# First modulation weights in four chunks of columns, with the first row pair multiplied chunk by chunk, in a hybrid encoder layer

## Chip, cores and metric

One core of one Trainium2 chip. The metric is device time in microseconds (us) from start to end of one launch of the whole layer; the median of three runs of the kernel before is 2013.69 us (2010.76 to 2014.69).

## What is computed

Two sequences (s = 0, 1) of 1024 rows by 1024 columns go through one encoder layer. What matters here is its beginning:

```
mod = silu(c) @ w_ada + b_ada                     # c: one vector of 1024 per sequence, w_ada: 1024 x 6144
sh1, sc1, ga1, sh2, sc2, ga2 = split(mod, 6)
h = rmsnorm(x, g_mix) * (1 + sc1) + sh1           # 1024 x 1024
z = h @ w_in                                      # to 448 latent columns (q_lat, kv_lat, k_pe) and 512 Fourier columns
...                                               # latent attention, 2-D Fourier mixing, w_out, residual, SwiGLU FFN
```

No row of `z` can be made before `sh1` and `sc1` are there, and these take the first 2048 columns of `w_ada`: 8 MB. All arithmetic is in float32. Matrix products are made from high and low parts with three matmuls each (`mm3`, lines 79 to 81).

## The kernel before

The whole kernel is one program. The order of the work on each engine is the order in which the program issues it, except where a scheduler moves an instruction forward; `tc.issue_after(x)` and `behind()` hold an instruction back until `x`, or the last split, was issued. SyncE (SP) issues almost all loads of this part in one queue, strictly in order: a load that waits for its buffer holds back all loads after it. TensorE (PE), VectorE (DVE), ScalarE (ACT) and GpSimd (POOL) also keep their order. Tiles with the same `tag` share a buffer, so a load into a tag waits until the earlier tile's readers are done.

The part that is changed is the opening, up to the second pair of row blocks:

- **Modulation.** `mod_load(c, ...)` loads rows 128c to 128c+127 of the first 2048 columns of `w_ada` (1 MB, eight times), and `mod_mm(0, c, ...)` makes four matmuls of 512 columns from it, one for each group of 512 columns (L233). They add over c, so the result is complete only when the eighth block is in. Then `modrow` is copied from PSUM (L655), four transposes (L160) turn it into columns, and `mod_vecs` (L163, L166) makes the scales `s1` and the shifts `sh1`.
- **Weights folded meanwhile.** Between the loads, `fold_q`, `fold_out` (L269, L270), `prep_wcs` (L352 to L362, the Fourier weights `wcs`) and `wz_split` prepare weights.
- **First pair (k = 0).** A pair is 128 rows and their 128 partners. `norm(k)` squares the rows on ACT (L383), takes the inverse root on POOL (`rstd`, six small operations, L104 to L111) and scales the rows on DVE (L396). `flip(k, g)` transposes two blocks of 128 columns of both row blocks (L424), and ACT applies `s1` and `sh1` (L431). For k = 0 the result is split into `hh` and `hl`, and `zproj` multiplies both row blocks by `wz` (24 matmuls of 448 columns each). `evenodd` makes sums and differences of the two row blocks on POOL (L452) and splits them; `fourier_in(k, 0)` and `fourier_in(k, 1)` multiply them by `wcs` (24 matmuls of 280 columns, 24 of 256).
- **Second pair (k = 1).** It is flipped between the parts of the first; `latents` transposes the first pair's normalised latents (L538); then `zboth(1)` multiplies sum and difference by `wz` (i = 0, 24 matmuls; i = 1, 24 matmuls). Between these two lie the transposes of the inverse roots of the third pair (L404, in `prepare`).

Of the kernel before, what the change touches and what calls it, by code (L numbers as in the profile page):

```python
# [12 lines left out]
F32 = mybir.dt.float32  # L13
# [40 lines left out]
def hybrid_encoder_kernel(ctx: ExitStack, tc: tile.TileContext, a: dict):  # L54
# [72 lines left out]
    s1 = [edge.tile([P, NC], F32, name=f"s1_{s}") for s in range(2)]  # L127
    sh1 = [const.tile([P, NC], F32, name=f"sh1_{s}") for s in range(2)]
# [51 lines left out]
    with ExitStack() as st:  # L180
# [14 lines left out]
        wuqT = w.tile([P, HEADS, QL], F32, tag="hh0", name="wuqT")  # L195
        wq = w2.tile([P, 4, 512], F32, tag="wada", name="wq", bufs=2).rearrange("p a b -> p (a b)")[:, :1536].rearrange("p (a b) -> p a b", a=2)
# [31 lines left out]
        def mod_mm(key, c, wt):  # L228
            if c == 0:
                mods[key] = bank()  # L230
            for n, j in enumerate((2, 3, 0, 1)):
                with tc.issue_after(here["m"]) if n else ExitStack():
                    here["m"] = nc.tensor.matmul(  # L233
                        mods[key][32 * j : 32 * j + 32, :], scT[:, c, :], wt[:, j, :], start=(c == 0), stop=(c == NC - 1)).ins

# [149 lines left out]
        def norm(k):  # L385
# [9 lines left out]
            for u in range(2):  # L395
                nc.vector.tensor_scalar(out=xt[u], in0=xt[u], scalar1=r[:, u : u + 1], scalar2=None, op0=ALU.mult)  # L396

# [13 lines left out]

        def flip(k, g):
            s, j = pairs[k]
            if g == 0:
                st1["hf", k] = w3.tile([P, NC, 2, P], F32, tag="hf", name="hf", bufs=1)
                if k == 0:
                    st1["hh", k] = w.tile([P, NC, 2, P], F32R, tag="hh0", name="hh")
                    st1["hl", k] = w.tile([P, NC, 2, P], F32R, tag="hl0", name="hl")
            hf, xt = st1["hf", k], st1["x", k]
            pt = bank().rearrange("p (c u t) -> p c u t", c=2, u=2)  # L420
            for c in range(2):
                for u in range(2):
                    cc = 2 * g + c
                    nc.tensor.transpose(pt[:, c, u, :], xt[u][:, cc * P : (cc + 1) * P], ident)  # L424
            for c in range(2):
                cc = 2 * g + c
                if k == 0 and cc == 1:
                    nc.vector.tensor_scalar(out=hf[:, cc], in0=pt[:, c], scalar1=s1[s][:, cc : cc + 1],
                                            scalar2=sh1[s][:, cc : cc + 1], op0=ALU.mult, op1=ALU.add)
                    continue  # L430
                nc.scalar.activation(hf[:, cc], pt[:, c], AF.Identity, bias=sh1[s][:, cc : cc + 1], scale=s1[s][:, cc : cc + 1])  # L431
            if k == 0:
                gs = slice(2 * g, 2 * g + 2)
                split(st1["hh", k][:, gs], st1["hl", k][:, gs], hf[:, gs])

        def evenodd(k, root=None):
# [3 lines left out]
            if k % 2 == 1:  # L440
                both = [w.tile([P, 2, NC, P], F32R, tag=f"h{t}1", name=f"eo{t}") for t in "hl"]
            for i, op in enumerate((ALU.add, ALU.subtract)):
                f = hf[:, :, 0, :] if i else w.tile([P, NC, P], F32, tag="eo", name="eo", bufs=1)
                if k % 2 == 1:
                    fh, fl = both[0][:, i], both[1][:, i]
                else:
                    fh = w.tile([P, NC, P], F32R, tag=f"eoh{i}", name="eoh", bufs=1)
                    fl = w.tile([P, NC, P], F32R, tag=f"eol{i}", name="eol", bufs=1)
                for g in range(2):
                    gs = slice(4 * g, 4 * g + 4)  # L450
                    with tc.issue_after(root) if root is not None and i == 1 else ExitStack():
                        nc.gpsimd.tensor_tensor(out=f[:, gs], in0=hf[:, gs, 0, :], in1=hf[:, gs, 1, :], op=op)  # L452
# [7 lines left out]
        def zproj(k, u):  # L460
            hh, hl_ = st1["hh", k], st1["hl", k]
            pz = bank()
            for c in range(NC):
                mm3(pz[:, :DZ], hh[:, c, u, :], hl_[:, c, u, :], wz_h[:, c, :], wz_l[:, c, :], c == 0, c == NC - 1)
            mz = tiny.tile([P, 4], F32, name="mz")
            z_square(pz, mz[:, :2])
# [1575 lines left out]
```

## Time and profile before

| | |
|---|---|
| median of three runs | 2013.69 us |
| the profiled execution | 2015.8 us, with a span of 2014.0 us in the profile |
| mean granted TensorE clock | 0.996 |
| PE busy over the span | 1974.3 us, 98% |
| DVE, ACT, POOL busy | 1392.1, 889.1, 852.5 us |
| DMA over the span | 376.59 MB, mean 187 GB/s |

Times inside the profile are microseconds from the start of the span. A row of a timeline gives start, duration, engine, line, operation, the tiles (out<-in) and a count, and in brackets the idle time ahead and what ended it. "PEclk" is the TensorE clock that was granted, as a share of full speed. float32 matmuls appear as two instructions in the profile.

### The profile page before, as it was taken

What the parts mean: (1) busy time and instruction counts of PE and PEld (TensorE: products, weight loads), DVE (VectorE), ACT (ScalarE), POOL (GpSimd) and SP (SyncE); (2) the same over time, 40 slices, a digit from 0 to 9 for tenths busy, and PEclk for the clock granted to TensorE, in tenths of its full rate; (3) what the DMA queues carried; (4) which work ended last, traced back from release to release, by engine and by line L of the source; (5) the groups of instructions that cost most, each with busy time, mean ns of one, the idle gap of its engine ahead of it and who ended that gap; (6) DMA issues with size and microseconds to landing.
All of it is one profiled execution on the core that took longest, in us unless ns stands there. A gap on an engine that the chain in (4) does not pass through costs nothing.

```text
span 2014.0 us, 27568 instructions
## 1 busy us (share of the span) xinstructions
PE 1974.3 (98%) x9526; PEld 1619.1 (80%) x9526; DVE 1392.1 (69%) x2064; ACT 889.1 (44%) x1720; POOL 852.5 (42%) x1012
## 2 busy tenths in 40 slices
PE   7899999999999999999999999999999999999998
PEld 3788778888888877888888888888888888888886
DVE  4567757766677678777777667788755655656794
ACT  2675435555565564333333356453333333335541
POOL 0654312111223237878879410344644554420152
PEclk8999999999999999999999999999999999999999
DMA  9696884445543575555555497665332333257762
GB/s 393 256 329 205 278 319 115 126 94 126 142 116 114 179 267 199 193 174 194 197 161 197 171 309 244 223 229 181 126 103 97 110 101 104 100 198 247 250 227 86
DMA packets 179449, 376.59 MB, mean 187 GB/s; under 512 B 17996, under 2 KB 57548, under 8 KB 175468
## 3 DMA queue, kind: packets, MB, share of 16 engines
q1 hardware_dynamic: 156908, 305.60, 45.1%
q0 software_dynamic: 21824, 68.17, 11.1%
q8 instruction: 75, 1.23, 0.3%
q10 hardware_dynamic: 576, 1.05, 0.1%
q14 instruction: 66, 0.54, 0.1%
HBM read 262.75 MB, written 120.39 MB: 190 GB/s over the span
## 4 chain that ended last, share of the span: by engine, by line
PE 57%; DVE 3%; issue 1%; POOL 1%; DMA 1%; ACT 0%; SPq 0%; POOLq 0%; DVEq 0%; ACTq 0%
PE bank L80 19%; PE bank L79 19%; PE bank L81 19%; DVE wl L64 1%; DMA draw<-s_d 1%; DVE val L152 0%; DVE val L1806 0%; DVE val L1834 0%; DVE val L1725 0%; DVE H L64 0%; POOL rs_y L107 0%; ACT wh L63 0%; DVE val L149 0%; POOL out_dram L1840 0%; DVE val L1708 0%
## 5 line engine op out<-in xcount | busy, mean ns | idle before, releaser
L79 PE MATMUL bank<-H,wh 128*128 128x512 f32 x1232 | 480.7, 390 | 3.2 <-DVE val L152 1.4
L80 PE MATMUL bank<-H,wh 128*128 128x512 f32 x1232 | 479.7, 389 | 0.3 <-DVE H L64 0.3
L81 PE MATMUL bank<-H,wl 128*128 128x512 f32 x1232 | 479.6, 389 | 0.2 <-DVE wl L64 0.2
L79 PEld LDWEIGHTS bank<-H,wh 128*128 128x128 f32 x1232 | 231.3, 188 | 54.7 <-DVE val L152 2.7
L81 PEld LDWEIGHTS bank<-H,wl 128*128 128x128 f32 x1232 | 231.3, 188 | 48.7 <-DVE wl L64 0.5
L64 DVE TENSOR_TENSOR wl<-draw,wh 128x512 fp32r<-128x512 f32 x286 | 206.7, 760 | 92.1 <-ACT wh L63 91.7
L80 PEld LDWEIGHTS bank<-H,wh 128*128 128x128 f32 x1232 | 231.3, 188 | 48.0 <-DVE H L64 0.6
L152 DVE TENSOR_TENSOR val<-bank,val 128x512 f32<-128x512 f32 x200 | 136.6, 689 | 160.4 <-PE bank L81 159.4
L63 ACT CAST wh<-draw 128x512 fp32r<-128x512 f32 x286 | 165.4, 619 | 174.7 <-PE bank L80 136.2
L152 POOL TENSOR_TENSOR val<-val 128x512 f32<-128x512 f32 x58 | 82.0, 1415 | 344.4 <-DVE val L1806 162.3
L80 PE MATMUL bank<-wl,wh 128*128 128x512 f32 x572 | 223.4, 391 | 1.4 <-DVE wl L64 1.4
L79 PE MATMUL bank<-wh 128*128 128x512 f32 x572 | 222.8, 390 | 0.0
L81 PE MATMUL bank<-wh,wl 128*128 128x512 f32 x572 | 222.7, 389 | 0.0
L63 ACT CAST wh<-rgu 128x512 fp32r<-128x512 f32 x172 | 107.1, 622 | 258.8 <-PE bank L80 203.2
L63 ACT CAST wh<-val 128x512 fp32r<-128x512 f32 x133 | 82.3, 621 | 261.0 <-PE bank L80 247.0
L64 DVE TENSOR_TENSOR wl<-val,wh 128x512 fp32r<-128x512 f32 x133 | 131.0, 987 | 67.4 <-ACT wh L63 67.4
L64 DVE TENSOR_TENSOR wl<-rgu,wh 128x512 fp32r<-128x512 f32 x172 | 163.8, 952 | 0.7 <-ACT wh L63 0.7
L149 POOL TENSOR_TENSOR val<-rgu 128x512 f32<-128x512 f32 x80 | 107.6, 1345 | 79.4 <-DMA rgu<-in_wgu_dram 75.6
L80 PEld LDWEIGHTS bank<-wl,wh 128*128 128x128 f32 x572 | 107.4, 188 | 25.8 <-DVE wl L64 3.6
L79 PEld LDWEIGHTS bank<-wh 128*128 128x128 f32 x572 | 107.4, 188 | 22.7 <-ACT wh L63 0.3
L81 PEld LDWEIGHTS bank<-wh,wl 128*128 128x128 f32 x572 | 107.4, 188 | 22.1
L149 POOL TENSOR_TENSOR val<-val 128x512 f32<-128x512 f32 x89 | 119.3, 1359 | 1.3
(400 smaller groups left out, 3901.6 us busy)
## 6 DMA issues: line engine op xcount, KB each, us to landing
rgu<-in_wgu_dram SPq DMA_DIRECT2D x86, 512.0 KB, 4.0
draw<-s_d SPq DMA_DIRECT2D x143, 256.0 KB, 3.1
s_d<-val POOLq DMA_DIRECT2D x88, 256.0 KB, 3.0
draw<-t_d SPq DMA_DIRECT2D x88, 256.0 KB, 4.4
s_d<-val SPq DMA_DIRECT2D x66, 256.0 KB, 3.7
draw<-in_w_down_dram SPq DMA_DIRECT2D x55, 256.0 KB, 4.0
wada<-in_w_ada_dram SPq DMA_DIRECT2D x11, 1024.0 KB, 10.3
xt<-in_x_dram SPq DMA_DIRECT2D x16, 512.0 KB, 10.2
```

What stands on the lines that cost most here:

```text
L63: here["a"] = nc.scalar.copy(hi, src).ins
L64: here["v"] = (eng or nc.vector).tensor_tensor(out=lo, in0=src, in1=rd(hi), op=ALU.subtract).ins
L79: nc.tensor.matmul(out, lh, rh, start=first, stop=False, skip_group_check=cont)
L80: nc.tensor.matmul(out, lh, rl, start=False, stop=False, skip_group_check=cont)
L81: here["t"] = nc.tensor.matmul(out, ll, rh, start=False, stop=last, skip_group_check=cont).ins
L149: return eng.tensor_tensor(out=out, in0=x, in1=y, op=ALU.subtract).ins
L152: eng.tensor_tensor(out=out, in0=x, in1=y, op=ALU.add)
```

## The change

The 2048 columns of `w_ada` come in a new layout, in four chunks of 512 columns (256 of shift, the same 256 of scale) over all 1024 rows: two loads of 1 MB for each chunk g (`cols_load(g, i)`). `cols_mm(g)` makes eight matmuls (L248), after which the chunk's 256 columns of `s1` and `sh1` can be finished by `cols_vecs(g)`: a copy (L253), four matmuls of two columns that add up the partial sums and turn them into columns (L256), and four small DVE operations (L263 to L267). Then `flip(0, g)` and `first_part(g)` follow: the 24 matmuls of this quarter (12 of 448 columns, 6 of 280, 6 of 256), before the next chunk's `cols_mm` is complete.

Sums and differences of the two row blocks are made from the normalised rows before the transposes (`xe` on DVE, `xt[0]` on POOL, inside `norm`), for k = 0 and k = 1. `flip` then writes the split halves `eh`, `el`, `oh`, `ol` itself, and `evenodd` and `zproj` are not called for these pairs. The latents of pair 0 are finished by `z_finish`, as for later pairs. Buffers are given out anew: the second half of chunk 2 takes tag `hl0`, which `prep_wcs(4)` to `prep_wcs(7)` read until then; heads 2 and 3 of `fold_out` move behind `first_part(3)`, and their four stores to `wo_d` behind `x_load(3)`.

```diff
+        def cols_load(g, i, t):
+            nc.sync.dma_start(t, a["wada1"][g, i].rearrange("p (c n) -> p c n", n=512))
+            return t
+
+        def cols_mm(g, ts):
+            ps = mods["g", g] = bank()
+            for i in range(2):
+                for n, j in enumerate((2, 3, 0, 1)):
+                    with tc.issue_after(here["m"]) if n else ExitStack():
+                        here["m"] = nc.tensor.matmul(
+                            ps[32 * j : 32 * j + 32, :], scT[:, 4 * i + j, :], ts[i][:, j, :], start=(i == 0), stop=(i == 1)).ins
+
+        def cols_vecs(g):
+            mr = stile("modrow")
+            nc.vector.tensor_copy(mr, mods.pop(("g", g)))
+            pt = bank()[:, :8].rearrange("p (b s) -> p b s", b=4)
+            for b in range(4):
+                nc.tensor.matmul(pt[:, b, :], mr[:, b * P : (b + 1) * P], sel, start=True, stop=True)
...
@@ norm
+            xe = w.tile([P, D], F32, tag="eo", name="xe", bufs=1)
+            for g in range(2):
+                gs = slice(512 * g, 512 * g + 512)
+                add(xe[:, gs], xt[0][:, gs], xt[1][:, gs], nc.vector)
+                sub(xt[0][:, gs], xt[0][:, gs], xt[1][:, gs], nc.gpsimd)
@@ flip
-                nc.scalar.activation(hf[:, cc], pt[:, c], AF.Identity, bias=sh1[s][:, cc : cc + 1], scale=s1[s][:, cc : cc + 1])
...
+                nc.scalar.activation(hf[:, cc, 0], pt[:, c, 0], AF.Identity, bias=dsh[:, cc : cc + 1], scale=s1[s][:, cc : cc + 1])
+            for c in range(2):
+                cc = 2 * g + c
+                here["o"] = nc.scalar.activation(oh[:, cc], pt[:, c, 1], AF.Copy, scale=s1[s][:, cc : cc + 1]).ins
+                nc.vector.scalar_tensor_tensor(out=ol[:, cc], in0=pt[:, c, 1], scalar=s1[s][:, cc : cc + 1],
+                                               in1=rd(oh[:, cc]), op0=ALU.mult, op1=ALU.subtract)
+            gs = slice(2 * g, 2 * g + 2)
+            split(eh[:, gs], el[:, gs], hf[:, gs, 0, :])
@@ the opening
-        mod_mm(0, 6, wt[0])
-        mod_mm(0, 7, wt[1])
...
-        zproj(0, 0)
...
+        def first_part(g):
+            for mm, ps in ((z_mm, pz), (f_mm, pc)):
+                for i in range(2):
+                    for c in range(2 * g, 2 * g + 2):
+                        mm(0, ps if mm is z_mm else ps[i], i, c)
+
+        cols_mm(0, wt[0])
+        cols_vecs(0)
+        flip(0, 0)
+        for i in range(4, 6):
+            prep_wcs(i, wf[i // 2])
+        wt.append([cols_load(2, i, wide(f"h{'hl'[i]}0")) for i in range(2)])
+        first_part(0)
+        for i in range(6, 8):
+            prep_wcs(i, wf[i // 2])
+        cols_mm(1, wt[1])
+        cols_vecs(1)
+        flip(0, 1)
+        wt.append([cols_load(3, i, wada_tile()) for i in range(2)])
+        first_part(1)
+        x_load(1)
+        wo2.append(wo_load(1, wide("hl0", (P, 2, D))))
...
+        cols_mm(2, wt[2])
+        cols_vecs(2)
+        flip(0, 2)
+        first_part(2)
...
+        cols_mm(3, wt[3])
+        cols_vecs(3)
+        flip(0, 3)
+        with behind(), tc.issue_after(here["o"]):
+            norm(1)
+        x_load(2)
...
+        first_part(3)
+        with tc.issue_after(here["t"]):
+            for h in (2, 3):
+                fold_out(h, wo2[1], wuvT, [wo2[1][:, h % 2, 512 * g : 512 * g + 512] for g in range(2)])
```

On PE, before, between the last weight preparation and the first product of pair 0 (L233 is the modulation matmul, L160 the transposes of `modrow`, L424 those of the rows):

```order
L269 MATMUL bank<-wide,wuvT 128x512 x2
L352 MATMUL bank<-c_138,wf 128x128 x8
L233 MATMUL bank<-wide,scT 32x512 x4
L233 MATMUL bank<-wada,scT 32x512 x4
L160 MATMUL bank<-ident,modrow 128x128 x4
L424 MATMUL bank<-ident,xt 128x128 x16
L79 MATMUL bank<-wz_h,hh 128x448
```

On PE, now, around chunk 1 (L385 is `prep_wcs`, L248 the modulation matmul of a chunk, L256 the four small matmuls, L468 the transposes of the rows):

```order
L385 MATMUL bank<-c_136,wide 128x128 x8
L248 MATMUL bank<-wide,scT 32x512 x8
L256 MATMUL bank<-wq,modrow 128x2 x4
L468 MATMUL bank<-ident,xe 128x128
L468 MATMUL bank<-ident,xt 128x128
L468 MATMUL bank<-ident,xe 128x128
L468 MATMUL bank<-ident,xt 128x128
L248 MATMUL bank<-wide,scT 32x512 x4
L79 MATMUL bank<-wz_h,eoh 128x448
```

What was one run of transposes behind all modulation matmuls is now four rounds; the first four modulation matmuls of chunk 2 stand ahead of chunk 1's products, the other four behind all 24 of them, and so again for chunk 3.

On SP, now, the loads of the chunks with what each waits for (L375 is `wz`, L240 a half chunk, L639 the Fourier weights; DMAHW is an earlier load's end, and the last five rows are chunk 1's second half, chunk 2 and chunk 3):

```order
L375 DMA wide<-in_wz_dram 128x1792 [waits DMAHW4_49]
L240 DMA wada<-in_wada_dram 128x2048 [waits DMAHW5_49]
L240 DMA wada<-in_wada_dram 128x2048 [waits DMAHW6_49]
L639 DMA wide<-in_wfT_dram 128x1024 [waits DMAHW7_49]
L639 DMA wide<-in_wfT_dram 128x1024 [waits DMAHW0_49]
L240 DMA wide<-in_wada_dram 128x2048 [waits DMAHW3_49,DMAHW1_49,DVE_49]
L240 DMA wide<-in_wada_dram 128x2048 [waits DMAHW4_49,DMAHW2_49,DVE_49]
L240 DMA wide<-in_wada_dram 128x2048 [waits PE_49]
L240 DMA wide<-in_wada_dram 128x2048 [waits DMAHW7_49,DMAHW0_49,PE_49]
L240 DMA wada<-in_wada_dram 128x2048 [waits DMAHW5_49]
L240 DMA wada<-in_wada_dram 128x2048 [waits DMAHW6_49]
```

The load that waits for `DMAHW7_49,DMAHW0_49,PE_49`, the second half of chunk 2, now has to wait for PE to finish `prep_wcs(7)`, which stands behind `first_part(0)`; before, the Fourier weights lay in buffers (tags `eoh` and `eol`) that no load of modulation weights uses.

On POOL, now, the second pair's way to its flips (L111 ends the `rstd` of pair 1's rows, L104 to L111 on `mz` is the `rstd` of pair 0's latents, L150 the two differences of pair 1's rows):

```order
L111 TENSOR_TENSOR rs_r<-rs_w,rs_y 128x2
L104 TENSOR_SCALAR rs_v<-mz 128x4
L107 TENSOR_TENSOR rs_y<-rs_v,mhalf 128x4
L108 TENSOR_TENSOR rs_w<-rs_y 128x4
L109 TENSOR_TENSOR rs_w<-rs_w,rs_v 128x4
L110 TENSOR_SCALAR rs_w<-rs_w 128x4
L111 TENSOR_TENSOR rs_r<-rs_w,rs_y 128x4
L150 TENSOR_TENSOR xt<-xt 128x512 x2
```

Before, the flips of pair 1 needed no POOL operation after the `rstd` of their rows; now the differences come first, and they stand behind the `rstd` of pair 0's latents.

More of the change, by code (lines that the diff above doesn't have):

```diff
@@ L458, in evenodd @@
                 yield
[L460 to L466, printed above, removed]
-            z_out(k, u, pz, stile("lat"), rstd(mz[:, :2], 2))
         def zboth(k, between):
-            eo = st1["eo", k]
             pz = [bank() for _ in range(2)]
-            mz = tiny.tile([P, 4], F32, name="mz")
             if 3 < k + 2 < nk:
@@ L629, in hybrid_encoder_kernel @@
+        pz, pc = ([bank() for _ in range(2)] for _ in range(2))
+        def first_part(g):
+            for mm, ps in ((z_mm, pz), (f_mm, pc)):
+                for i in range(2):
+                    for c in range(2 * g, 2 * g + 2):
[3 more added lines that the diff above has]
+        flip(0, 0)
         for i in range(4, 6):
             prep_wcs(i, wf[i // 2])
-        mod_mm(0, 4, wt[0])
-        mod_mm(0, 5, wt[1])
-        with tc.issue_after(here["m"]):
-            fold_out(3, wo2[1], wuvT, pair_of("eol0"))
-            for i in range(6, 8):
-                prep_wcs(i, wf[i // 2])
@@ L683, in first_pair @@
             next(more, None)
-            latents(0, 1)
             next(more, None)
```

176 lines of the change are left out of this document (85 added, 91 removed).

## Prediction

> **What bounds the kernel now.** I read the engines' shares first, then the span in stretches, since only the opening is changed.
>
> ```profile
> PE 1974.3 (98%) x9526; PEld 1619.1 (80%) x9526; DVE 1392.1 (69%) x2064; ACT 889.1 (44%) x1720; POOL 852.5 (42%) x1012
> ```
> ```profile
> 0.00:24.00 24.00, 18.05 (x81) 9.90 (x82) 8.48 (x23) 3.25 (x8) 1.69 (x9) 1.00 0.93 361
> 24.00:44.50 20.50, 15.30 (x80) 6.42 (x79) 10.02 (x25) 8.65 (x23) 1.73 (x6) 0.83 1.02 424
> 44.50:61.50 17.00, 14.00 (x69) 12.75 (x70) 10.25 (x20) 11.19 (x24) 4.61 (x9) 0.90 0.97 371
> 61.50:84.10 22.60, 17.08 (x116) 13.39 (x114) 12.94 (x30) 12.78 (x29) 15.05 (x28) 1.00 0.49 162
> 84.10:160.00 75.90, 75.90 (x475) 62.83 (x472) 48.54 (x114) 50.63 (x125) 45.61 (x86) 1.00 0.85 312
> ```
>
> The columns are stretch, length, busy time of PE, its weight loads, DVE, ACT and POOL, then granted clock, DMA share, GB/s. From 84.1 on PE is never idle, so what counts is when PE gets there: at the second half (i = 1) of `zboth(1)`. Ahead of it PE idles 19.7 us (84.1 less 18.05, 15.30, 14.00 and 17.08). Until 61.5 the DMA engines are full. PE's own waits:
>
> ```profile
> PE bank L233 <- DMA wide<-in_w_ada_dram: 4.0, 2, 2.4
> PE bank L538 <- DVE lat L514: 3.4, 2, 1.8
> PE bank L404 <- POOL rs_r L111: 1.5, 1, 1.5
> ```
> ```profile
> 9.27 1.93 PE L233 MATMUL bank<-wada,scT 128*32 128x512 f32 x6 [1.22 <-DMA wada<-in_w_ada_dram]
> ...
> 30.48 1.07 PE L233 MATMUL bank<-wide,scT 128*32 128x512 f32 x8 [1.61 <-DMA wide<-in_w_ada_dram]
> 33.94 1.93 PE L233 MATMUL bank<-wide,scT 128*32 128x512 f32 x8 [2.40 <-DMA wide<-in_w_ada_dram]
> ...
> 43.41 1.06 PE L233 MATMUL bank<-wada,scT 128*32 128x512 f32 x8 [1.00 <-DMA wada<-in_w_ada_dram]
> 46.65 1.08 PE L160 MATMUL bank<-ident,modrow 128*128 128x128 f32 x4 [2.18 <-DVE modrow L655]
> ...
> 61.49 0.29 PE L79 MATMUL bank<-wcs_h,eoh 128*128 128x280 f32 x1
> ...
> 64.59 1.04 PE L424 MATMUL bank<-ident,xt 128*128 128x128 f32 x8
> ...
> 72.07 0.38 PE L79 MATMUL bank<-wcs_h,eoh 128*128 128x256 f32 x1
> ...
> 75.24 0.47 PE L79 MATMUL bank<-wz_h,eoh 128*128 128x448 f32 x1
> ...
> 84.06 0.47 PE L79 MATMUL bank<-wz_h,eoh 128*128 128x448 f32 x1
> ...
> 89.03 0.29 PE L79 MATMUL bank<-wcs_h,eoh 128*128 128x280 f32 x1
> ```
>
> The opening is bound by loads up to 43.41, then by one chain through all engines (clock drops included: the same four modulation matmuls take 1.07 and 1.93).
>
> **The loads.** 1,897 KB (from the tiles' shapes) were in at 9.27 and 10,665 KB at 30.48: 413 KB per us. The change loads the same bytes before the last modulation matmul, but in its queue 8,361 KB end with chunk 0: 9.27 + 6,464/413 = 24.9. Chunk 1 (11,433 KB) comes at 32.4. Chunk 2's second half waits for `prep_wcs(7)`, and chunk 3, the second pair's rows and everything else on SP queue behind it.
>
> **One chunk's chain.** PE keeps its order, so a chunk's second four modulation matmuls start only when the 24 products of the chunk before are done, and every step after them waits for the last one.
>
> ```profile
> 45.82 0.68 DVE L655 COPY modrow<-bank 128x512 f32<-128x512 f32 x1
> 47.77 0.17 DVE L163 TENSOR_TENSOR sh<-bank,pk 128x8 f32<-128x8 f32 x1 [1.27 <-PE bank L160]
> ...
> 48.33 0.17 DVE L166 SCALAR_TENSOR_TENSOR s<-s,pk 128x8 f32<-128x8 f32 x1
> ```
> ```profile
> 48.68 0.56 ACT L431 ACTIVATE hf<-bank,sh,s 128x256 f32<-128x256 f32 x1 [3.65 <-PE bank L424]
> ```
> ```profile
> L1213 ACT ACTIVATE ht<-pht,sh,s 128x128 f32<-128x128 f32 x96 | 34.8, 472 | 8.7 <-PE pht L1210 8.7
> ...
> L878 ACT CAST qsk<-qt 128x256 fp32r<-128x256 f32 x16 | 6.5, 409 | 2.2 <-POOL qt L876 2.2
> ```
> ```profile
> 26.85 2.02 PE L352 MATMUL bank<-c,wf 128*128 128x128 f32 x16 [0.16 <-DVE so L270]
> ```
>
> - Modulation matmuls: 1.07.
> - Copy of `modrow`: 0.05 + 0.68 + 0.15 to PE (46.50 to 46.65): 0.88.
> - Four small matmuls: no row has two columns. Between 0.54 (four transposes, 1.08 at half clock) and 1.01 (half of the eight in the 2.02 row): 0.75, since they are plain float32 matmuls like the upper end but with less to stream.
> - DVE: six such operations took 0.73 (47.77 to 48.50), so four take 0.55. PE's transposes run beside them.
> - ACT: 0.18 to start, three operations of 34.8/96 = 0.36, a cast of 0.41, 0.1 to PE: 1.78.
> - 24 products: 12/24 of 4.97 (84.06 to 89.03), 6/24 of 3.10 (61.49 to 64.59) and of 3.17 (72.07 to 75.24): 4.05.
>
> Sum 9.08 per chunk; low ends 8.5. The next chunk's first four matmuls lie in the wait for ACT and cost nothing.
>
> **Chunk by chunk.** Chunk 0: PE has waited long, so its second half at 24.9 runs at half clock, 1.93, to 26.8; copy 27.7; small matmuls 1.5, 29.2; transposes 1.0, 30.2; then `prep_wcs(4)` and `(5)` stand ahead of the products: 2.02 to 4.04 by the clock, taken at 2.5 as PE hardly pauses after 24.9: 32.7. Products to 36.8; `prep_wcs(6)` and `(7)` 2.02 to 38.8. Now chunk 2's second half may load: 1 MB is 2.5 us and some start, in by 43.5 and used at 49: hidden, by 5 us; the DMA engines idle some 4 us for it, which they can afford, since chunk 3 is used only at 58. Chunk 1: 38.8 + 1.07 + 9.08 = 48.95. Chunk 2: 58.0. Chunk 3: T = 67.1. (Before, the products of pair 0 ended at 75.2, but with the second pair's flips and the latents' transposes between them.)
>
> **From T to the second pair.**
>
> ```profile
> 15.41 3.80 PE L269 MATMUL bank<-wide,wuvT 128*128 128x512 f32 x8
> ```
> ```profile
> 35.15 1.06 ACT L383 ACTIVATE junk<-xt 128x1024 bf16<-128x1024 f32 x1 [4.04 <-DMA xt<-in_x_dram]
> ...
> 36.43 1.06 ACT L383 ACTIVATE junk<-xt 128x1024 bf16<-128x1024 f32 x1
> ```
> ```profile
> 37.67 0.24 POOL L104 TENSOR_SCALAR rs_v<-ms 128x2 f32<-128x2 f32 x1 [35.39 <-ACT junk L383]
> ...
> 39.62 0.20 POOL L111 TENSOR_TENSOR rs_r<-rs_w,rs_y 128x2 f32<-128x2 f32 x1
> ...
> 73.33 1.29 POOL L452 TENSOR_TENSOR hf<-hf 128x512 f32<-128x512 f32 x1
> ...
> 98.24 0.23 POOL L104 TENSOR_SCALAR rs_v<-mz 128x4 f32<-128x4 f32 x1
> ...
> 100.53 0.20 POOL L111 TENSOR_TENSOR rs_r<-rs_w,rs_y 128x4 f32<-128x4 f32 x1
> ```
>
> `fold_out` fills PE to T + 3.8. Pair 1's squares follow chunk 3's ACT work, about T - 3.7, with a PSUM copy between them: to T - 0.6. Its `rstd` (2.15) ends at T + 1.5, the latents' `rstd` (2.5, after their squares at T + 1.75) at T + 4.3, and only then come the differences, 1.3 each: T + 5.7 and T + 7.0. PE idles 2 us, flips (0.52 each) to T + 8.2. ACT then needs 4 x (4 x 0.36 + 0.41) = 7.4 for them, from T + 6.4 to T + 13.8, and DVE scales the latents between its parts of the third and fourth flip, so the latents' transposes (2 x 0.52) end at T + 13.7. One modulation round 1.07; i = 0 of `zboth(1)` from T + 14.8 to T + 19.8. The third pair's squares start behind the latents' casts, T + 15, so its `rstd` is ready at T + 19.7: no wait is left of the 1.5. Transposes 0.4 and a modulation round 1.07: i = 1 at T + 21.3 = 88.4, where it was 84.06: **+4.3**.
>
> **The clock.**
>
> ```profile
> 28.90:33.90 5.00, 1.07 (x8) 0.16 (x8) 1.46 (x5) 1.35 (x5) 0.00 (x0) 0.88 1.01 415
> 42.40:46.60 4.20, 1.07 (x9) 0.16 (x8) 4.11 (x9) 2.00 (x5) 0.00 (x0) 0.97 1.02 421
> 65.60:70.50 4.90, 1.54 (x13) 1.30 (x13) 3.09 (x10) 2.32 (x9) 3.98 (x15) 1.00 0.09 27
> ```
>
> The first two stretches, with PE busy 1.07 of 5.0 and of 4.2, lost the clock; 1.54 of 4.9 didn't. Chunks 1 and 2 have 2.3 of 4.0 between their modulation matmuls and their products: safe. Chunk 3 has no next chunk to fill with: 1.2 of 4.0. Before the second latents PE is busy 0.5 of 5.0. A loss costs up to 2.7 (0.86 at 33.94 and 1.9 of the `fold_out` behind it). I take half of one, +1.4, between 0 and 5.4. The Trainium skill, "TensorE: Matmul & The Clock Gate", "HAM oscillation", gives as abstract rule that PE must have no idle gap over about 3.4 us; no gap here is as long except ahead of chunk 0, so by it this term would be 0 and the sum +4.3. The trace differs: its longest gap in the first two stretches is 2.40.
>
> **Behind it.** From 84 on the same matmuls run, so the shift stays unless a load comes late. The nearest is that of the third pair's transposed rows:
>
> ```profile
> 85.38 2.48 DVE L407 TENSOR_TENSOR xT<-xT,bank 128x512 f32<-128x512 f32 x4 [4.54 <-DMA xT<-in_xt_dram]
> ```
>
> DVE had it 1.3 us after i = 1 began, and PE did not idle. Now SP issues it behind the latents' stores, about T + 16 = 83, with the DMA engines nearly idle: in by about 88, again within 1 us of i = 1. Cost 0; if it is 3 us late, `zboth(2)` starts up to 3 us late, which the range holds. The four moved stores to `wo_d` (1 MB, 2.5 us of DMA) stand ahead of the fourth pair's rows, needed some 15 us later: 0.
>
> **Sum:** +4.3 + 1.4 = +5.7. The profiled execution's 2015.8 would become 2021.5; it lies 2.1 above the median of the runs, 2013.69, which becomes **2019.4**.
>
> **Rivals.**
> - *Short ends.* Small matmuls 0.54, `prep_wcs` at full clock, no clock lost: -0.8, -0.5, -1.4 and 0.8 less on small ACT operations, +2.2; with -1 to +4 around it, 2016. For it: chunk 0's clock is a guess. Against: each end would have to be short.
> - *The loads set the pace* (faster): each chunk's small steps run beside the products of the one before. Chunk 3 is in at 9.27 + 13,632/413 = 42.3, T = 51.4, i = 1 at 72.7: -10, 2003.7. For it: full DMA until 61.5. Against: the order on PE above, and the load behind `prep_wcs(7)`. It decides if a chunk takes under 5.8 us, not 9.08.
> - *Half clock in every chunk:* three more losses of 2.7, +13.8, 2027.5. Against: the next chunk's matmuls fill the waits.
>
> **Chances.** Forecast (+4 to +9) 0.52, short ends 0.30, loads 0.10, half clock 0.08. A difference under 0.2% (4.0 us) can't be told from none. Slower 0.60, same 0.30, faster 0.10. The range holds forecast, most of the short ends, and the low part of half clock: 2011 to 2026.
>
> **What would show it.** Right: in PE's timeline the products of the four chunks end near 37, 49, 58 and 67, with a `modrow` copy of 0.68 and ACT in each wait; POOL's differences end near 74; PE is without idle from 88. Wrong first: if chunk periods are 6 to 7 us (a step hidden that I put on the path), if chunk 0's products end before 33, or if the loads behind chunk 2 come after their use at 58.

## The result, and the profile after

The changed kernel is slower: 2030.86 us in the median of four runs (2026.45 to 2031.88), against 2012.84 us for the kernel before beside it (2010.76 to 2014.69); ratio 1.0086, 95% interval 1.0067 to 1.0104. The direction was forecast, the size was not: +18 us instead of +5.7, and outside the range. The profiled execution took 2031.3 us with a span of 2029.5, 15.5 more than the one of before, and that difference is what the traces can explain.

Two of the prediction's stretches, in its columns:

```profile
24.00:44.50 20.50, 16.20 (x93) 12.59 (x93) 10.95 (x27) 5.08 (x17) 0.00 (x0) 0.70 0.54 206
...
61.50:84.10 22.60, 16.71 (x67) 12.79 (x68) 13.22 (x40) 12.25 (x40) 8.18 (x18) 0.77 0.50 190
```

In 24 to 44.5 the DMA engines are half idle (0.54, before 1.02) and the granted clock is 0.70 (0.83); in 61.5 to 84.1 the clock is 0.77 where it was 1.00. Three of PE's own waits between 20 and 240 (total, times, longest):

```profile
PE bank L256 <- DVE modrow L253: 5.9, 4, 3.5
PE bank L79 <- DVE nyl L64: 5.8, 1, 5.8
...
PE bank L79 <- ACT eoh L474: 1.6, 3, 1.2
```

The waits for `modrow` and `eoh` are the small steps of the chunks. The second line was in nobody's forecast: 5.8 us for `nyl`, a tile of the Fourier stage, some 140 us behind the opening. PE's timeline of the chunks, and the second half of `zboth(1)`:

```profile
23.93 1.93 PE L248 MATMUL bank<-wada,scT 128*32 128x512 f32 x8 [1.28 <-DMA wada<-in_wada_dram]
29.33 1.86 PE L256 MATMUL bank<-wq,modrow 128*128 128x2 f32 x8 [3.47 <-DVE modrow L253]
...
31.95 3.62 PE L385 MATMUL bank<-c,wide 128*128 128x128 f32 x16
...
39.77 1.95 PE L385 MATMUL bank<-c,wide 128*128 128x128 f32 x16
...
51.24 1.06 PE L248 MATMUL bank<-wide,scT 128*32 128x512 f32 x8
...
59.97 1.07 PE L248 MATMUL bank<-wada,scT 128*32 128x512 f32 x8
...
71.32 3.60 PE L302 MATMUL bank<-wide,wuvT 128*128 128x512 f32 x8
```
```profile
93.23 0.47 PE L79 MATMUL bank<-wz_h,eoh 128*128 128x448 f32 x1
```

The products of the chunks end where the next work begins: 39.77, 51.24, 59.97 and 71.32 (forecast 36.8, 48.95, 58.0, 67.1), and the second half of `zboth(1)` begins at 93.23, 9.2 later than the 84.06 of before. DVE ahead of chunk 0's copy:

```profile
19.40 2.63 DVE L308 TENSOR_SCALAR wq<-lq,pk 128x256 f32<-128x256 f32 x2
...
25.60 3.08 DVE L64 TENSOR_TENSOR wz_l<-wide,wz_h 128x896 fp32r<-128x896 f32 x3
28.60 0.68 DVE L253 COPY modrow<-bank 128x512 f32<-128x512 f32 x1
```

The copy of `modrow` begins at 28.60, though its matmuls ended at 25.86 (23.93 + 1.93): DVE still had work ahead of it in its queue, among it the scalings of `wpe` (2.63) and the low parts of `wz` (3.08 for the last three).

Then the end of the stage. The latents are split into a high part (a cast on ACT) and a low part (on DVE) in a tile `lhl`, which SP stores to `lat_d`. ACT's first cast of the Fourier stage's tile `A`, and SP's last stores of `lhl`; then the same two of before:

```profile
236.36 0.65 ACT L63 CAST A<-bank 128x256 fp32r<-128x256 f32 x2 [8.76 <-DMA lat_d<-lhl]
```
```profile
229.04 2.68 SPq L564 DMA_DIRECT2D lat_d<-lhl  x2
```
```profile
217.76 0.65 ACT L63 CAST A<-bank 128x256 fp32r<-128x256 f32 x2 [0.31 <-ACT wnh L1024]
```
```profile
215.93 1.42 SPq L529 DMA_DIRECT2D lat_d<-lhl  x2
```

Before, the cast came 0.31 us behind the work ahead of it. After, ACT sat 8.76 us until a store from `lhl` to `lat_d` had landed. The built programs give these tiles the following places (bytes of a partition):

```
                              before            after            e1                 e9 to e11
lhl, last pair (tag)          11776-19968 (hh0) 97536-105728 (hh0) 134400-142592 (hl0) 134400-142592 (hl0)
lhl, pairs before (lq, two)   93440-101632      89344-97536      89344-97536        13824-22016
e2: as before, but lhl of the last pair at 101632-109824 (hl0)
A of the stage behind: A0 (high part, written by ACT) 95744-99840, A1 (low part, written by DVE) 99840-103936
B (B0 and B1): 103936-112128 in all
```

`wuqT` was the pool's first tile and had the tag `hh0`, so `hh0` lay at the pool's start. The change gives `wuqT` the tag `eo`, `hh0` is then placed behind the others, and the last latents come to lie under `A` and `B`.

To tell where time is lost, a *shift* is used below: each DVE instruction of the kernel before that begins in a stretch, against the instruction of the same operation, tile and shape with the same place from the end, and the median of these differences.

| kernel | shift at 120 to 140 | at 240 to 260 | span | median | ratio to before |
|---|---|---|---|---|---|
| after | 9.3 | 16.0 | 2029.5 | 2030.86 | 1.0086 [1.0067, 1.0104] |
| e1 last tile moved | 9.1 | 10.6 | 2024.1 | 2025.98 | 1.0056 [1.0041, 1.0071] |
| e2 before, tile moved | -0.1 | -0.7 | 2011.8 | 2013.49 | 0.9997 [0.9988, 1.0007] |
| e3 DVE first | 5.5 | 6.8 | 2020.5 | 2021.97 | 1.0036 [1.0023, 1.0049] |
| e4 one ahead | 4.6 | 6.5 | 2020.4 | 2019.53 | 1.0026 [1.0017, 1.0036] |
| e5 tail order | 10.4 | 21.1 | 2033.6 | 2035.61 | 1.0109 [1.0094, 1.0124] |
| e6 second load first | 1.6 | 2.9 | 2016.2 | 2019.87 | 1.0030 [1.0019, 1.0040] |
| e7 ahead and tail | 0.2 | 5.3 | 2019.0 | 2020.78 | 1.0036 [1.0023, 1.0050] |
| e8 rows early | -0.4 | 7.6 | 2020.8 | 2021.59 | 1.0034 [1.0020, 1.0048] |
| e9 all tiles moved | 7.3 | 8.1 | 2021.2 | 2023.73 | 1.0051 [1.0037, 1.0065] |
| e10 latents behind | -8.5 | -5.9 | 2008.5 | 2010.79 | 0.9984 [0.9975, 0.9993] |
| e11 ACT scales | -8.9 | -8.1 | 2005.0 | 2009.05 | 0.9972 [0.9962, 0.9983] |

So the changed kernel loses 9.3 in the opening and 6.7 between 140 and 240; behind that the shift hardly moves (15.8 at 2000).

### The profile page after: what moved, and what is told of

Read it like the earlier page. It is cut to its first block, busy times and chain, and to the rows that moved or that the text cites. A ratio compares the mean times of both kernels' runs of the same rounds, so it can differ in the third digit from the quotient of the medians.

```text
span 2029.5 us, 27642 instructions
## 1 busy us (share of the span) xinstructions
PE 1982.7 (98%) x9554; PEld 1629.6 (80%) x9554; DVE 1395.3 (69%) x2097; ACT 886.7 (44%) x1734; POOL 843.2 (42%) x1002
## 4 chain that ended last, share of the span: by engine, by line
PE 55%; DVE 4%; issue 2%; DMA 1%; POOL 1%; ACT 0%; SPq 0%; POOLq 0%; DVEq 0%; ACTq 0%
PE bank L80 18%; PE bank L79 18%; PE bank L81 18%; DVE wl L64 1%; DVE val L1851 1%; DMA draw<-s_d 0%; DVE val L153 0%; DVE H L64 0%; DMA val<-x_d 0%; DVE val L1879 0%; DVE val L1770 0%; ACT wh L63 0%; POOL rs_y L107 0%; POOL val L153 0%; DVE val L150 0%
## 5 line engine op out<-in xcount | busy, mean ns | idle before, releaser
L64 DVE TENSOR_TENSOR wl<-val,wh 128x512 fp32r<-128x512 f32 x133 | 123.0, 927 | 66.9 <-ACT wh L63 66.9
L150 POOL TENSOR_TENSOR val<-rgu 128x512 f32<-128x512 f32 x80 | 108.3, 1354 | 80.6 <-DMA rgu<-in_wgu_dram 76.8
L150 POOL TENSOR_TENSOR val<-val 128x512 f32<-128x512 f32 x89 | 118.9, 1355 | 1.3
```

The lines of the kernel that those rows point to most:

```text
L64: here["v"] = (eng or nc.vector).tensor_tensor(out=lo, in0=src, in1=rd(hi), op=ALU.subtract).ins
L150: return eng.tensor_tensor(out=out, in0=x, in1=y, op=ALU.subtract).ins
```

## The experiments

### e1: the last latents in another tile

```diff
-                    st1["lhl"] = w.tile([P, 4, 512], F32R, tag="hh0", name="lhl")
+                    st1["lhl"] = w.tile([P, 4, 512], F32R, tag="hl0", name="lhl")
```

> The changed kernel, with one name changed: the last pair's split latents (`lhl`) go into the tile of the tag hl0 instead of hh0, so that in memory they lie under other tiles of the next stage (hl0 is at bytes 134400 to 142592 of a partition, hh0 at 97536 to 105728, and the next stage's `A` and `B` at 95744 to 108032). Every engine's order of instructions stays the same. Theory M (memory): the change gave the tag hh0 another place, the Fourier stage's first tile `A` now lies over the last latents, and PE's 5.8 us wait for `nyl` at 230 is the store of these latents; it goes, and the span falls from 2029.5 to 2023.5 to 2025. Theory O (order): the stores are late because ACT and DVE take the latents in another order, and `A` waits for the pair before as well: the wait stays at 4 or more, and the span falls by less than 2 us. In both the second half of zboth(1) still begins at 93.2.

PE's wait for `nyl`, and ACT's first cast of `A`:

```profile
PE bank L79 <- DVE nyl L64: 1.1, 1, 1.1
```
```profile
231.55 0.65 ACT L63 CAST A<-bank 128x256 fp32r<-128x256 f32 x2 [4.10 <-DMA lat_d<-lhl]
```

Theory M holds: the wait fell from 5.8 to 1.1 and the span by 5.4, with the same order on every engine up to 245 us, so a renamed tile cost 5.4 us of span. 4.7 of it are the wait; behind the long wait the changed kernel's matmuls also ran slower for a while (0.63 us for one of 512 columns, 0.40 in the kernel before). The medians of the timed runs lie 4.9 apart, and their ranges overlap. What is left is a wait of 4.10 on ACT for a store of `lhl` too, now that of a pair before (`lq` lies under `A0`), which PE feels little. Up to the end of chunk 3 this run is the changed kernel; its rows are compared with those of e9 below.

### e2: the same move in the kernel before

The same edit, in the kernel before.

> The kernel before, with the same name changed (last `lhl` in hl0). There hl0 lies at bytes 101632 to 109824 of a partition, under `A` and `B` of the next stage (95744 to 112128), while hh0 (11776 to 19968) is free of them. Theory M (memory): the kernel before gets the wait that the changed one has. Its last latents' stores are issued at 215.93 and land some 4.2 us after issue, about 221.5, where the first `A` is written at 217.8: 3 us longer, between 1.5 and 5, with a cast of `A` or its low part (DVE) released by the store. Theory O (order): the orders of before are kept, so nothing changes: within 0.5 us.

DVE's first write to the low part of `A`:

```profile
221.63 0.76 DVE L64 TENSOR_TENSOR A<-bank,A 128x256 fp32r<-128x256 f32 x2 [0.19 <-DMA lat_d<-lhl]
```

Theory M missed: nothing is lost (ratio 0.9997). But the wait is there: this write now waits for the store, for 0.19 us, up to 221.63; DVE was busy with other splits until 221.44. The edit is that of e1, but the place is not that of the changed kernel: here the latents lie under `A1` and `B` alone, so the first write over them is DVE's, while in the changed kernel they lie under `A0` too, whose first write is ACT's cast. In the kernel before that cast comes at 217.76; over these stores it would have waited until some 221.4, 3.7 us by an estimate from these rows, and no run shows what PE would have felt of it. So e2 shows only that a place costs nothing where its first write comes no earlier than the store lands. After the change two things meet: the place under `A0`, and stores issued at 229.04 where the shift alone would make it 225.2 (215.93 + 9.3), 3.8 later.

### e3: DVE's queue ahead of chunk 0

On top of e1 (in outline):

```diff
-        fold_pe(wpe)                        # ahead of chunk 0
...
         flip(0, 0); prep_wcs 4, 5; first_part(0)
+        with tc.issue_after(here["q"]):     # q: the last write to eol in flip
+            fold_pe(wpe)
```

> The changed kernel with the last latents moved as in the first run, and on DVE the two scalings of `wpe` (2.63 us together) moved from ahead of chunk 0's copy of `modrow` to behind its products' inputs. Theory S (one serial chain): DVE's queue held chunk 0's copy (28.60, while its matmuls ended at 25.86), so the copy starts at 26.0 and everything after it up to the second half of zboth(1) comes 2.6 us earlier (1.5 to 3): products of chunk 0 start at 32.6, that second half begins near 90.6, span 2.6 below that of the first run. Theory C (clock): what chunk 0 loses it loses by the half clock of PE (its small matmuls and weight products took twice as long), which a shorter wait doesn't change, or the waits for loads take the gain back: less than 0.8 us at the second half of zboth(1).

PE's rows, first one of e1, then e3's:

```profile
28.90 1.86 PE L256 MATMUL bank<-wq,modrow 128*128 128x2 f32 x8 [3.41 <-DVE modrow L253]
```
```profile
27.83 1.87 PE L256 MATMUL bank<-wq,modrow 128*128 128x2 f32 x8 [1.72 <-DVE modrow L253]
...
39.42 1.92 PE L248 MATMUL bank<-wide,scT 128*32 128x512 f32 x16
...
62.42 0.47 PE L79 MATMUL bank<-wz_h,eoh 128*128 128x448 f32 x1 [1.19 <-ACT eoh L474]
...
66.45 3.60 PE L302 MATMUL bank<-wide,wuvT 128*128 128x512 f32 x8
```

The wait for `modrow` fell by 1.7, and chunk 1's modulation matmuls came at 39.42 instead of 41.13 in e1: theory S holds, with 1.7 for the forecast 2.6, because `wz_l` stays in the queue. The end of chunk 3's products moved more, by 4.3 (70.77 to 66.45). The other 2.6 are the clock: its first product took 0.47 here, and 0.74 in e1, behind the same wait (e1's rows stand under e9). At the second half of `zboth(1)` 3.2 of the 4.3 are left (92.78 to 89.55).

### e4: one chunk ahead

On top of e3, `prep_wcs` 4 to 7 and the next chunk's steps are written ahead of a chunk's products (in outline, for each g):

```diff
+        cols_mm(g + 1, wt[g + 1]); cols_vecs(g + 1); flip(0, g + 1)
         first_part(g)
```

> As the run before, and the chunks are taken one ahead: all four remaining weight products (prep_wcs 4 to 7) follow chunk 0's transposes, and a chunk's modulation matmuls, copy, vectors and transposes are written ahead of the 24 products of the chunk before it, so that these products run beside the small steps. Theory S (serial chain): the period of a chunk falls from 9 to 11 us to about 6 (products 4.05, four plus four modulation matmuls 2.1), the products of chunk 3 end near 54 (50 to 58) instead of 71.3, the second half of zboth(1) starts near 75 (70 to 80), ahead of the 84.06 of the kernel before, and the span is below 2014 by 4 to 12 us, if the later loads keep up. Theory L (loads): chunk 2's and 3's loads, issued at 26.7 to 43, set the pace, and products wait for them whatever the order: chunk 3's products end no earlier than 64, the second half of zboth(1) not before 85, the span about 2018 to 2022.

PE (chunk 2's and chunk 3's modulation, the end of the products, the second half of `zboth(1)` and the next round of the other modulation), and SP's queue:

```profile
46.26 1.92 PE L248 MATMUL bank<-wide,scT 128*32 128x512 f32 x16
...
53.54 1.92 PE L248 MATMUL bank<-wada,scT 128*32 128x512 f32 x16
...
64.62 3.60 PE L302 MATMUL bank<-wide,wuvT 128*128 128x512 f32 x8
...
83.85 0.45 PE L79 MATMUL bank<-wz_h,eoh 128*128 128x448 f32 x1
...
88.08 1.07 PE L236 MATMUL bank<-wada,scT 128*32 128x512 f32 x8 [1.74 <-DMA wada<-in_w_ada_dram]
```
```profile
79.51 2.28 SPq L564 DMA_DIRECT2D lat_d<-lhl  x2
81.83 0.66 SPq L226 DMA_DIRECT2D wada<-in_w_ada_dram  x1
```

The period fell to 7.3 (46.26 to 53.54; 8.7 to 11.4 in the changed kernel), not to 6: PE is busy all of 44.5 to 61.5, and the small matmuls (0.95) and transposes are work of PE too, which theory S forgot. The products end at 64.62: S's 50 to 58 is missed, and L's number (not before 64) is met, as is its span, but not for its reason, since PE waits for no load between chunk 0 and the end of the products. Then the second half of `zboth(1)` begins at 83.85, as early as before, and the gain is given back behind it: PE waits 1.74 at 88.08 for weights whose second half SP issued only at 81.83, behind the stores of the latents. Against e3 nothing is left in the span: 2020.4 and 2020.5.

### e5: copies, squares and kv splits in the order of before

In the changed kernel, with `lhl` left in `hh0`:

```diff
+            with after_these("kv") if k == nk - 1 else ExitStack():   # a, v of the pair before's kv split
                 z_square(...)
...
+            with after_these("l1") if k == nk - 2 else ExitStack():   # a, v of the latents ahead of it
                 split(kv[:, 0, :], kv[:, 1, :], sk[:, QL : QL + KVL])
```

> The changed kernel with its last latents where the change put them (tag hh0, under `A` and `B`), but with the order of the kernel before at the end of the stage: on ACT and DVE the last copies and squares come behind the `kv` splits of the pair before, and these behind the split latents of the pair before that. Theory B (both are needed): the first run showed that the lying of the tile costs 5.4 us, the second that it costs nothing when the stores are as early as before. Then the order alone takes the wait away too: the last stores are issued near 225 instead of 229, land near 230, where `A`'s low part is written anyway, PE's wait for `nyl` falls from 5.8 to under 1.5, and the span from 2029.5 to 2023 to 2025. Theory M (the memory alone): the wait stays above 4 and the span above 2027.

```profile
211.87 0.59 ACT L63 CAST lhl<-bank 128x512 fp32r<-128x512 f32 x1 [5.22 <-DMA lat_d<-lhl]
```
```profile
225.18 1.94 PE L585 MATMUL bank<-ident,lat 128*128 128x128 f32 x8 [2.93 <-DVE lat L558]
```

Theory B's forecast missed: 4 us slower instead of 5 faster. The wait for `nyl` is gone from PE's list, but ACT, now held to that order, sits 5.22 us at a cast of `lhl` until an earlier store from the same buffer has landed, DVE and PE follow, and PE waits 2.93 for the latents. An order forced from outside replaced one wait by larger ones. M's forecast missed as well (the wait was to stay above 4), so the run does not decide between them.

Where the stores become late can be read from the two kernels themselves. SP's first store of the pair before the last and the DVE split that matters to it, after the change and before it:

```profile
224.45 2.42 SPq L564 DMA_DIRECT2D lat_d<-lhl  x2
```
```profile
225.65 0.68 DVE L64 TENSOR_TENSOR lhl<-bank,lhl 128x512 fp32r<-128x512 f32 x1
```
```profile
211.93 1.27 SPq L529 DMA_DIRECT2D lat_d<-lhl  x2
```
```profile
211.21 1.45 DVE L64 TENSOR_TENSOR lhl<-bank,lhl 128x512 fp32r<-128x512 f32 x2 [0.20 <-ACT lhl L63]
```

SP stores the pair before the last first, then the last pair, in both kernels. But in the built programs the splits changed places: before, ACT and DVE split the pair before the last first; after, the last pair. So the second of these two stores waited for a split that ended at 226.33 (225.65 + 0.68), and before for one that ended at 212.66: 13.7 later, 4.4 more than the shift. From there to the last stores it is 2.7 us after the change (229.04) and 3.3 before (215.93), so SP's queue adds nothing. The order of the splits makes the stores late, then; this is read from traces and programs, and no run tests it, since e5's program still has the last pair's splits first. Why the scheduler turned them stays open.

### e6: the second load first

On top of e4:

```diff
             small_weights()
+            second = mod_load(1, cols1, wada_tile())
             yield
...
-                if c + 1 < NC:
+                if c == 0:
+                    nxt = second
+                elif c + 1 < NC:
```

> The fourth run's kernel (one chunk ahead), and the second round's weights of the other modulation (cols1, c = 1) are asked for with the `w4` weights, so that on SP all of it stands ahead of the first latents' stores; in the fourth run its second half was issued only at 81.8, behind stores that waited for the latents, PE waited 1.7 for it at 88 and ran at half clock behind. Theory Q (SP's queue): the shift against the kernel before, 1.6 at 60 and 4.6 at 100, stays at 0 to 2 at 100, and the span falls from 2020.4 by 3 to 4.5, to about 2016.5. Theory L (loads): the next load is late in its place (the third pair's transposed rows or the round after), and the span falls by less than 1.5.

```profile
60.41 1.01 SPq L226 DMA_DIRECT2D wada<-in_w_ada_dram  x2
```

Theory Q holds in the profile: both parts are issued at 60.41, ahead of the stores (76.89), PE's wait is gone, the shift at 100 to 120 is 1.6 instead of 4.6, the span 4.2 less. The timed runs don't show it: 2019.87 against 2019.53 in the median, with the runs of both together from 2015 to 2023. So single spans of these kernels say less than a wait in them does.

### e7: both

e6 with the edit of e5.

> The run before with the order of the kernel before at the end of the stage, as in the run ahead of it. Theory B: the rest of the late stores goes (PE's wait of 1.0 for `nyl`, the shift of 1.9 between 200 and 240), the span is 1 to 2 below that of the run before, near 2014.5, within 0.1% of the kernel before. Theory M: nothing changes, within 0.5.

Neither: the shift rises from 0.2 at 120 to 5.3 at 240, by 5.1, where e6 has 1.3. It is e5's result again, in another kernel.

### e8: the second pair's rows early

On top of e7:

```diff
         flip(0, 2)
+        with behind(), tc.issue_after(here["o"]):
+            norm(1)                          # xe in a tile of hh0
         first_part(1)
...
         flip(0, 3); first_part(2)
+        flip(1, 0); flip(1, 1)
         first_part(3)
+        flip(1, 2); flip(1, 3)
```

> The run before, and the second pair's norm follows chunk 2's transposes instead of chunk 3's (its sum of rows goes into a tile of hh0, since the first pair's is still read), and its transposes and modulation stand ahead of and behind chunk 3's products instead of behind `fold_out`. Theory S (serial chain): the stretch from the end of chunk 3's products to the first product of zboth(1), 13.6 us in the fourth run (64.6 to 78.2), falls to 7 to 10, the second half of zboth(1) begins at 77 to 80, and the span is 3 to 6 below that of the run before, near 2010, below the kernel before. Theory L (loads): from 84 on the loads have no slack for an earlier start (their share was 0.85 to 1.0), PE waits for weights or rows there, and the span falls by less than 1.5.

```profile
72.19 1.76 PE L591 MATMUL bank<-ident,lat 128*128 128x128 f32 x7 [4.40 <-DVE lat L564]
...
76.46 0.74 PE L85 MATMUL bank<-wz_h,eoh 128*128 128x448 f32 x1
...
83.51 0.47 PE L85 MATMUL bank<-wz_h,eoh 128*128 128x448 f32 x1
```

`zboth(1)` begins at 76.46, 1.8 earlier than in e4, and its second half at 83.51 instead of 77 to 80: both theories missed. Pair 1 is ready, but PE's order has the first pair's latents ahead of `zboth(1)`, and PE waits 4.40 for them. Between 120 and 240 the shift rises by 8.0 (-0.4 to 7.6), 2.9 more than in e7; no run here explains that.

### e9: nothing under A

On top of e1, `kv` and `lq` are the pool's first tiles:

```diff
+        pk = w.tile([P, 2, KVL], F32, tag="kv", name="pk", bufs=2)...
+        lq = [w.tile([P, 2, 512], F32, tag="lq", name="lq0", bufs=2) for _ in range(2)]
         wuqT = w.tile([P, HEADS, QL], F32, tag="eo", name="wuqT", bufs=1)
```

> The first run's kernel (the change, last latents in hl0), and the tiles `kv` and `lq` (the `lhl` of the pairs before) are allocated first in the pool, so that nothing whose store comes late lies under `A` and `B`; every engine's order stays. The first run left PE a wait of 1.1 for `nyl` and ACT one of 4.1 for a store of `lhl` at its first cast of `A`. Theory M (the memory): these go too, the shift against the kernel before stays at its value of 120 to 160 (9.1 to 9.3) up to the end, and the span is 1.0 to 1.6 below the first run's 2024.1. Theory O (order): what is left comes from ACT's and DVE's order and stays: within 0.5 of 2024.1.

The wait for `nyl` is gone, and between 120 and 240 the shift rises by 0.8 (7.3 to 8.1), after 1.5 in e1 and 6.7 in the changed kernel: theory M, with 0.7 for this step (forecast 1.0 to 1.6). The rest of the 2.9 by which the span fell is not the tiles'. Chunk 3's first product and `fold_out` behind the last, in e1 and in e9:

```profile
64.10 0.74 PE L79 MATMUL bank<-wz_h,eoh 128*128 128x448 f32 x1 [1.19 <-ACT eoh L474]
...
70.77 3.60 PE L302 MATMUL bank<-wide,wuvT 128*128 128x512 f32 x8
```
```profile
63.65 0.47 PE L79 MATMUL bank<-wz_h,eoh 128*128 128x448 f32 x1 [1.19 <-ACT eoh L474]
...
67.66 3.60 PE L302 MATMUL bank<-wide,wuvT 128*128 128x512 f32 x8
```

Same instructions, same wait, and 6.67 against 4.01 us for chunk 3's products: the first ran at half clock for the most part, the second didn't.

### e10: the latents behind

e6 with e8's early rows (without the edit of e5), e9's places, all latents' transposes held behind the last product issued (before, those of the first pair were not), and:

```diff
             def between(c):
+                if k == 1 and c == NC - 1:      # behind i = 0 of zboth(1)
+                    for u in range(2):
+                        latents(0, u)
...
+            xt_load(2)                          # ahead of the first latents' stores
+            x_load(3)
             next(z, None)
```

> The sixth run's kernel (one ahead, second load first) with the second pair's rows early as in the eighth run, the tiles moved as in the run before, the first pair's latents transposed behind the first half (i = 0) of zboth(1) instead of ahead of it, and the third pair's rows asked for ahead of the first latents' stores. In the eighth run PE waited 4.4 us (67.8 to 72.2) for these latents while the inputs of zboth(1) were there. Theory S (serial chain): zboth(1) begins at 69 to 71 instead of 76.5, its second half at 76 to 78, the shift against the kernel before is -4 to -8 at 120 and stays, the span is 2006 to 2010. Theory L (loads): the third pair's rows and the modulation's weights come no earlier, PE waits for them between 76 and 110, and the shift at 120 is -2 or more, the span about 2012.

```profile
63.64 3.60 PE L302 MATMUL bank<-wide,wuvT 128*128 128x512 f32 x8
...
68.16 0.47 PE L79 MATMUL bank<-wz_h,eoh 128*128 128x448 f32 x1
...
76.17 0.47 PE L79 MATMUL bank<-wz_h,eoh 128*128 128x448 f32 x1
```

Theory S holds at this place: `zboth(1)` begins at 68.16, its second half at 76.17, 7.9 earlier than in the kernel before, and PE waits only once more, 0.6, up to 110. The kernel is faster than the one before: 2010.79 against 2014.40 in the same runs, ratio 0.9984 (0.9975 to 0.9993). Of the -8.5 at 120 only -5.9 are left at 240, where S said that it would stay; the clock was 0.97 between 180 and 240 here, and 1.00 in e11, which keeps -8.1 of -8.9. The row of e10, then that of e11:

```profile
180.00:240.00 60.00, 57.67 (x342) 48.25 (x344) 45.18 (x96) 28.63 (x74) 17.70 (x30) 0.97 0.79 264
```
```profile
180.00:240.00 60.00, 57.87 (x350) 47.95 (x349) 45.70 (x96) 28.25 (x72) 17.13 (x29) 1.00 0.81 269
```

By an estimate from these rows (0.03 of 60 us) the clock is some 1.8 of the 2.6.

### e11: ACT scales

On top of e10:

```diff
+                if act:                         # heads 0 and 1
+                    nc.scalar.activation(outs[g], ps, AF.Copy, scale=gq[:, 2:3])
+                else:
                     nc.vector.tensor_scalar(out=outs[g], in0=ps, scalar1=gq[:, 2:3], scalar2=None, op0=ALU.mult)
```

> The run before, and the four scalings behind `fold_out` of heads 0 and 1 (1.40 us for two on DVE) are made by ACT, which idles from 20.8 to 32 there. Theory D (DVE's queue holds chunk 0): the copy of chunk 0's `modrow` comes at 25.9 to 26.2 instead of 27.6, the products of the chunks and zboth(1) 1.0 to 1.8 earlier than in the run before, the span 1 to 1.8 less. Theory C (clock or loads): PE then waits for chunk 1's or 2's load or loses the clock, and the gain is under 0.5.

```profile
19.30 6.24 DVE L64 TENSOR_TENSOR wz_l<-wide,wz_h 128x896 fp32r<-128x896 f32 x4
26.14 0.69 DVE L254 COPY modrow<-bank 128x512 f32<-128x512 f32 x1 [0.60 <-PE bank L249]
```
```profile
63.21 3.60 PE L302 MATMUL bank<-wide,wuvT 128*128 128x512 f32 x8
```

Theory D holds for the copy: it starts 0.60 us behind PE, at 26.14, and no longer behind DVE's queue (26.99 in e10). At `fold_out` 0.43 of these 0.85 is left (63.64 to 63.21), less than D forecast, as C said: the granted clock is a half until 32.9 in this trace and until 33.0 in e10's, so PE worked off the earlier start at half speed. 2009.05 us, ratio 0.9972 (0.9962 to 0.9983): 5.4 us faster than the kernel before in the same runs, and the fastest kernel here. Against e10 the intervals overlap; 1.7 us in the medians is not a measured gain.

## Why the prediction was right or wrong

**Right:** the chain itself. Chunk 2 took 8.73 (51.24 to 59.97) for 9.08, and T to the second half of `zboth(1)` 21.9 (71.32 to 93.23) for 21.3. Behind chunk 0 the loads were no bound: its second half came at 23.9 for 24.9, and e4's products ran without a wait for loads. POOL's differences wait behind the latents' inverse root, as said, and end 7.2 behind T for the forecast 7.0 (at 78.5, 76.01 + 2.49, instead of 74, because T came late):

```profile
72.94 0.44 POOL L104 TENSOR_SCALAR rs_v<-mz 128x4 f32<-128x4 f32 x1 [1.10 <-ACT junk L536]
...
76.01 2.49 POOL L150 TENSOR_TENSOR xt<-xt 128x512 f32<-128x512 f32 x2
```

**Wrong, first: "Chunk 0 ... to 26.8; copy 27.7".** The copy was put at PE's end, without asking what DVE had ahead of it. PE's matmuls ended at 25.86, 0.9 earlier than forecast, but the copy began only at 28.60, so the small matmuls came at 29.33 for 27.7, 1.6 late. e3 and e11 show DVE's queue as the cause, 1.7 us in e3. Half clock did the rest, 1.4: 3.3 to the first product from the start of `prep_wcs` 4 and 5 (31.95 to 35.22, forecast 2.5), and 4.55 for the products (forecast 4.05), the first of which ran slowly too. Chunk 0 ended 3.0 late (39.77 for 36.8).

**Wrong, second: the clock term, +1.4.** The term stood for chunk 3 and for the wait ahead of the second latents, as half of one loss. In this run the loss came in full: chunk 3's products took 6.74 (64.58 to 71.32) for 4.05, 2.7 more, which is the price that the prediction gives one loss. Chunk 3 in all took 11.35 (59.97 to 71.32), 2.25 over its forecast and within the term's bound of 5.4. Whether the loss comes is chance as far as the runs show: e1 has it and e9 hasn't, with the same work.

With the smaller misses (chunk 1 -0.7, chunk 2 -0.3, behind T +0.6) that makes 4.3 + 3.0 + 2.25 - 0.4 = 9.15, the measured 9.2.

**Wrong, third, and decisive: "Behind it ... Cost 0".** It asked which load would come late, and not which store, nor what lies under what. 6.7 of the 16 us come some 140 us behind the opening. Without them the forecast would have stood in its range: the opening's 9.2 alone give 2022.9. e1 shows 5.2 of the 6.7 as the place of one tile (its shift rises by 1.5 there), e9 0.7 more. The place turns late stores into time; that they come 3.8 us later than the shift is read from the order of the splits, and no run tests it (e5).

**The rivals.** *Short ends* failed at its first end: the small matmuls took 0.92 us to the transposes behind them (53.12 to 54.04), over the 0.75 taken and far from 0.54. Half clock in every chunk (2027.5) was nearest in time, for the wrong reason: chunks 1 and 2 ran at full clock. That the loads set the pace was wrong of this order of instructions; but what it described, small steps beside the products of the chunk before, is what e4 and e10 make of the same chunks, and e10's second half of `zboth(1)` at 76.17 is near its 72.7.

## What to carry to other kernels

When a step is cut into chunks, price the first chunk by the queue of each engine it enters, and write the next chunk's small steps ahead of this one's products, on every engine's order; otherwise each chunk pays the whole chain (8.7 us here at full clock, 7.3 one ahead). An edit that renames or reorders the first tiles of a pool moves the others: look up what the next stage's first tiles lie over, and which store or read lets go of that last. Follow a gain to the next wait: here e4's was given back to a load behind stores, e8's to latents ahead of products and e7's to a forced order.

## What the hardware showed unexpectedly

The granted clock is no function of the instructions and waits near it: chunk 3's products ran 6.67 us in e1 and 4.01 in e9, both behind the same wait of 1.19 us and with the same matmuls. In e1's trace the clock fell to a half at 63.1, in that wait, and for 6.8 us; in e9's it stayed whole until 76.1. In all traces here the stretches of half clock up to 250 us last 3.4, 6.8, 10.2 or 13.7 us, as if it were decided once in 3.4 us; that is read from the traces' clock records. The page "TensorE: Matmul & The Clock Gate" of the Trainium skill says, in "The HAM clock gate", that the window in which activity is counted runs free, so that the same kernel pays differently from run to run. The rows of e1 and e9 agree with that; the scatter of the changed kernel's runs (2026.45 to 2031.88) is compatible with it, but not traced. The page's abstract rule, no idle gap over some 3.4 us ("HAM oscillation"), does not cover chunk 3, whose longest gap was that 1.19.

A tile whose earlier content is still being stored delays its next writer until the store has landed, and only then: 8.76 us for ACT's first write after the change, 4.10 in e1, and 0.19 for DVE's later one in e2.
